# Two blocks of mixers and MLPs: the second layers' modulation vectors from VectorE, GpSimd and ScalarE instead of TensorE

## The chip, the cores and the metric

The kernel runs on one core of a Trainium2 chip. The metric is the time of one execution on the device in microseconds (us). Engines are named as in the profile: PE is TensorE, with PEld for its weight loads; DVE is VectorE, ACT ScalarE, POOL GpSimd; SP is the engine whose queue issues nearly all DMA loads.

## The reference, cut to what matters

There are two blocks of two layers each, on 256 tokens and 256 context tokens of width 1024. Every layer has a mixer and a squared-ReLU MLP (1024 to 4096 to 1024), each behind an RMS norm whose result is scaled and shifted by a modulation vector; another part of that vector scales what is added to the residual. Each layer has its own modulation matrix of 1024 x 6144, applied to two vectors: c for the tokens and c_ctx for the context.

```python
def modulation(cvec, w_mod, b_mod):
    m = (jax.nn.silu(cvec) @ w_mod + b_mod).reshape(-1, 1, N_MOD * D_MODEL)
    return jnp.split(m, N_MOD, axis=-1)

sh1, sc1, g1, sh2, sc2, g2 = modulation(c, w_mod[l], b_mod[l])
csh1, csc1, cg1, csh2, csc2, cg2 = modulation(c_ctx, w_mod[l], b_mod[l])
...
x = x + g1 * heads_out(att_x, px, hy, w_out[l])
x = x + g2 * sq_relu_mlp(modulate(rms_norm(x, norm2_g[l]), sh2, sc2), w_mlp1[l], w_mlp2[l])
```

The second block does the same with `ada_w`, `ada_b` and c_2, c_ctx_2; its first mixer is a gated DeltaNet, its second gated linear attention (GLA). In the last layer of each block only the tokens go through the MLP, so there are two MLPs with both streams (512 columns) and two with one (256 columns).

## The kernel before

The residual `xs` stays in SBUF, feature by feature, 8 tiles of 128 x 512 (tokens, then context). All large products are made in three passes of rounded fp32: a weight tile `wr` of 128x1024 comes by DMA, ACT rounds it to `wh` (line 296), DVE or POOL subtracts to get the rest `wl` (line 297), and PE multiplies wh by both parts of the input and wl by the first (lines 305 to 307). A weight has three buffers `wr`.

An MLP has four slabs. A slab takes eight weights up (each gives 128 hidden rows `h`: a relu on ACT from PSUM, a multiply on DVE for the square, then `pair` splits it into two rounded tiles `r` by an ACT cast and a DVE subtraction) and eight weights down, whose products are added to `xs` times the modulation (line 619). So an MLP has 64 weights. The weights' subtractions are on DVE, but for the first four, which are on POOL. The first products of an MLP with two streams begin while the norm of the second stream is still being made.

A modulation matrix is worked off in 48 steps (six groups of 1024 columns, eight slices of 128 rows each). A step loads 128x1024 values (`wm`, 512 KB) and has PE multiply them with silu(c) and silu(c_ctx) into PSUM `pmd`, four matmuls side by side in the array (line 365). After eight steps ACT copies the sums (`ev`), two more matmuls turn them feature-major and DVE adds the bias into `mod` (`moda` for the first block, `modb` for the second). The steps stand in a list; `pools` gives each stage a quota of them, and `background(n)` in the stages' code takes n of them. With four matrices there are 192 steps: 48 in layer 0's mixer, 24 in its MLP (10 ahead of the first products), 48 in layer 1's mixer (some run while its MLP begins), none in that MLP itself, 40 in DeltaNet (as 80 half steps: ten around the first heads and 70 in and behind the last head), 16 in the MLP behind DeltaNet and 16 in GLA.

A scheduler puts the instructions of each engine in an order at build time; at run time each engine works off its own list in order, and waits for what an instruction needs.

## Time and profile before

| what | value |
|---|---|
| three runs | 2713.63, 2722.64, 2725.65 us; median 2722.64 |
| profiled execution, first to last instruction (its span) | 2721.8 us |
| PE, DVE, ACT, POOL busy | 95%, 60%, 42%, 14% of the span |
| mean granted TensorE clock | 0.982 of full speed |
| DMA | 334 MB, mean 123 GB/s |
| first MLP with two streams | about 317 to 715 us |
| DeltaNet | about 1115 to 1935 us |
| second MLP with two streams | about 1935 to 2300 us |

The profile gives the execution's span; its time as a run isn't listed apart. The span lies 0.8 us below the median of the runs. Busy shares are means over stages of different kinds.

### The profile page before, as it was taken

The numbers are of one execution on the slowest core, as the hardware profiler recorded it, in microseconds if no ns is written. First come the engines' busy times: TensorE is split into PE (matmuls) and PEld (weight loads), VectorE is DVE, ScalarE is ACT, GpSimd is POOL, SyncE is SP. The second block draws the span as 40 slices with busy tenths as digits, with TensorE's granted clock in tenths as the row PEclk, the third lists the DMA queues.
The fourth block names the chain that finished last, engine by engine and source line by source line (L and its number), as shares of the span: only waits on it lengthen the run. The fifth ranks groups of instructions, "written<-read, shape, count | busy, mean of one in ns | idle before, by whom it ended". The sixth has DMA issues, their size and how long they took to land.

```text
span 2721.8 us, 41263 instructions
## 1 busy us (share of the span) xinstructions
PE 2583.2 (95%) x15900; PEld 2131.4 (78%) x15900; DVE 1629.2 (60%) x3455; ACT 1138.5 (42%) x2165; POOL 367.6 (14%) x270
## 2 busy tenths in 40 slices
PE   7999999999999999889999999999999999899999
PEld 5866777888866899867777787766778888687999
DVE  5554543344653678778776776775534445767675
ACT  3344332223443445545444444433422333563453
POOL 0000200000100101233232333322000002410100
PEclk9999999999999999999999999999999999999999
DMA  7234453223455656231112112236542222233554
GB/s 275 95 113 151 157 176 100 94 94 100 149 180 169 233 182 198 87 103 48 38 58 63 50 39 61 70 113 200 179 132 93 98 96 88 93 125 101 174 183 155
DMA packets 155205, 334.16 MB, mean 123 GB/s; under 512 B 60110, under 2 KB 71488, under 8 KB 155008
## 3 DMA queue, kind: packets, MB, share of 16 engines
q1 hardware_dynamic: 154752, 331.46, 37.3%
q8 instruction: 125, 2.05, 0.3%
q14 instruction: 72, 0.59, 0.1%
q0 software_dynamic: 256, 0.07, 0.0%
HBM read 327.79 MB, written 3.67 MB: 122 GB/s over the span
## 4 chain that ended last, share of the span: by engine, by line
PE 78%; DVE 13%; ACT 3%; DMA 3%; issue 2%; POOL 1%; SPq 0%; DVEq 0%; ACTq 0%
PE pmm L305 18%; PE pmm L306 18%; PE pmm L307 18%; PE pmd L365 3%; PE pt L986 1%; PE ps L958 1%; DVE lf L1211 1%; PE pv L994 1%; DMA wm<-amod 1%; PE pa L1280 1%; PE pa L1323 1%; PE pmm L324 1%; DVE Mt L1191 1%; PE pa L1275 1%; PE pa L1269 1%
## 5 line engine op out<-in xcount | busy, mean ns | idle before, releaser
L296 ACT CAST wh<-wr 128x1024 fp32r<-128x1024 f32 (+1 forms) x421 | 426.3, 1016 | 740.8 <-PE pmm L306 530.9
L305 PE MATMUL pmm<-h,wh 128*128 128x512 f32 (+2 forms) x1800 | 630.7, 351 | 18.2 <-DVE kq L1123 8.2
L307 PE MATMUL pmm<-h,wl 128*128 128x512 f32 (+2 forms) x1800 | 626.8, 348 | 14.3 <-DVE wl L297 9.4
L306 PE MATMUL pmm<-h,wh 128*128 128x512 f32 (+2 forms) x1800 | 627.2, 349 | 0.0
L297 DVE TENSOR_TENSOR wl<-wr,wh 128x1024 fp32r<-128x1024 f32 (+1 forms) x333 | 394.3, 1186 | 304.2 <-ACT wh L296 295.9
L305 PE MATMUL pmm<-r,wh 128*128 128x256 f32 (+1 forms) x1312 | 446.0, 341 | 11.6 <-DVE xs L619 10.1
L307 PE MATMUL pmm<-r,wl 128*128 128x256 f32 (+1 forms) x1312 | 444.1, 339 | 5.3 <-DVE wl L297 5.2
L306 PE MATMUL pmm<-r,wh 128*128 128x256 f32 (+1 forms) x1312 | 441.6, 337 | 0.4 <-DVE r L284 0.4
L297 POOL TENSOR_TENSOR wl<-wr,wh 128x1024 fp32r<-128x1024 f32 x88 | 214.2, 2437 | 1574.5 <-ACT wh L296 1169.5
L305 PEld LDWEIGHTS pmm<-h,wh 128*128 128x128 f32 x1800 | 343.6, 191 | 72.8 <-issue 11.3
L307 PEld LDWEIGHTS pmm<-h,wl 128*128 128x128 f32 x1800 | 345.0, 192 | 63.6 <-DVE wl L297 11.5
L306 PEld LDWEIGHTS pmm<-h,wh 128*128 128x128 f32 x1800 | 344.4, 191 | 46.0 <-issue 4.4
L305 PEld LDWEIGHTS pmm<-r,wh 128*128 128x128 f32 x1312 | 247.6, 189 | 53.8 <-issue 25.5
L307 PEld LDWEIGHTS pmm<-r,wl 128*128 128x128 f32 x1312 | 247.9, 189 | 30.7 <-DVE wl L297 6.1
L306 PEld LDWEIGHTS pmm<-r,wh 128*128 128x128 f32 x1312 | 248.2, 189 | 23.3 <-issue 1.6
L619 DVE SCALAR_TENSOR_TENSOR xs<-pmm,modb,xs 128x256 f32<-128x256 f32 x232 | 107.3, 478 | 127.2 <-PE pmm L307 126.9
L365 PE MATMUL pmd<-wm,cvs 128*32 128x256 f32 x1408 | 124.4, 394 | 10.3 <-DMA wm<-amod 7.0
L619 DVE SCALAR_TENSOR_TENSOR xs<-pmm,moda,xs 128x256 f32<-128x256 f32 x120 | 54.5, 479 | 130.1 <-PE pmm L307 130.0
L283 ACT CAST r<-h 128x256 fp32r<-128x256 f32 (+1 forms) x128 | 65.6, 514 | 135.8 <-DVE h L572 75.6
L284 DVE TENSOR_TENSOR r<-h,r 128x256 fp32r<-128x256 f32 (+1 forms) x128 | 72.7, 569 | 42.5 <-ACT r L283 39.8
L365 PEld LDWEIGHTS pmd<-wm,cvs 128*32 128x32 f32 x1408 | 36.4, 109 | 62.1 <-issue 25.6
L323 PE MATMUL pmm<-h,wh 128*128 128x256 f32 x224 | 63.7, 296 | 5.5 <-ACT h L480 3.8
(483 smaller groups left out, 3837.8 us busy)
## 6 DMA issues: line engine op xcount, KB each, us to landing
wr<-w SPq DMA_DIRECT2D x128, 512.0 KB
wr<-f SPq DMA_DIRECT2D x128, 512.0 KB
wm<-wmod SPq DMA_DIRECT2D x96, 512.0 KB
wm<-amod SPq DMA_DIRECT2D x56, 512.0 KB
wr<-dwin SPq DMA_DIRECT2D x49, 512.0 KB
...
```

The lines of the kernel that those rows point to most:

```text
L283: self.nc.scalar.copy(hi, src)
L284: self.nc.vector.tensor_tensor(lo, src, hi.bitcast(F32), ALU.subtract)
L296: self.nc.scalar.copy(hi, raw)
L297: (self.nc.gpsimd if pool or self.pool_lo else self.nc.vector).tensor_tensor(lo, raw, hi.bitcast(F32), ALU.subtract)
L305: mm(ps, wh[:, k, :], rh[:, n0:n1], start=k == 0, stop=False)
L306: mm(ps, wh[:, k, :], rl[:, n0:n1], start=False, stop=False)
L307: mm(ps, wl[:, k, :], rh[:, n0:n1], start=False, stop=k == last)
L323: mm(ps[:, c0:c1], wh[:, k, :], rh[:, c0:c1], start=k == 0, stop=False)
L324: mm(ps[:, c0:c1], wh[:, k, :], rl[:, c0:c1], start=False, stop=False)
L365: self.last = nc.tensor.matmul(ps[32 * c : 32 * c + 32, :256], cs[:, k, :], raw[:, 256 * j : 256 * j + 256], start=k == 0, stop=k == 7, ti ...
L619: self.nc.vector.scalar_tensor_tensor(x, ps, mod[:, 8 * gch + m, v : v + 1], x, ALU.mult, ALU.add)
L958: mm(ps[:, nk * i : nk * i + nk], q[:, C(b)], kp[hh % 2][:, k0:], start=True, stop=True)
```

## The change

The modulation matrices of the two second layers (`wmod_1` and `amod_1`) are laid out transposed on the host: 48 tiles of 128 output features by 1024 inputs. c and c_ctx are laid out repeated over the 128 partitions (`cb`, 2 x 1024 columns, put through Silu once on ACT). For each of the 48 tiles POOL multiplies it by silu(c_ctx) into a product `pr`, which ACT sums along its columns; DVE multiplies it by silu(c) and sums in one instruction (`jk` is its discarded product). Every eighth tile DVE adds the bias. This goes on during the two MLPs with two streams: `vec()` takes one tile after each hidden row block and after each of the first three slabs' down products. 96 steps on PE remain for the first layers' matrices: 48 in layer 0's mixer, 10 in its MLP ahead of the first products, 38 in layer 1's mixer; DeltaNet, the second MLP and GLA have none.

```diff
+def _rows(w):
+    return _c(w.T.reshape(48, P, 1024))
...
+    def modulation_v(self, wname, bname, cname, tag):
+        nc = self.nc
+        mod = self.cp.tile([P, 48, 2], F32, name="mod" + tag, tag="mod" + tag)
+
+        def steps():
+            cb = self.t("cb", 2048)
+            nc.sync.dma_start(cb, self.a[cname])
+            nc.scalar.activation(cb, cb, AF.Silu)
+            raws = []
+
+            def load(j):
+                raw = self.gp.tile([P, 1024], F32, tag="wm", bufs=self.nwm, name="wm")
+                nc.sync.dma_start(raw, self.a[wname][j])
+                raws.append(raw)
+
+            def total(j, prod):
+                nc.scalar.activation(prod, prod, AF.Copy, accum_out=mod[:, j, 1:2])
+                if j % 8 == 7:
+                    m = mod[:, j - 7 : j + 1, :]
+                    nc.vector.tensor_tensor(m, m, self.small(bname)[:, j - 7 : j + 1].unsqueeze(2).to_broadcast([P, 8, 2]), ALU.add)
+
+            late = None
+            for j in range(self.nwm):
+                load(j)
+            for j in range(48):
+                yield
+                raw = raws.pop(0)
+                prod = self.t("pr", 1024)
+                nc.gpsimd.tensor_tensor(prod, raw, cb[:, 1024:], ALU.mult)
+                jk = self.t("jk", 1024)
+                nc.vector.scalar_tensor_tensor(jk, raw, 1.0, cb[:, :1024], ALU.mult, ALU.mult, accum_out=mod[:, j, 0:1])
+                if j + self.nwm < 48:
+                    load(j + self.nwm)
+                if late:
+                    total(*late)
+                late = (j, prod)
+            yield
+            total(*late)
+
+        return mod, steps
...
+    def vec(self, n=1):
+        for _ in range(n):
+            if self.vs and next(self.vs, 0) == 0:
+                self.vs = None
...
+            if vs:
+                sb.update(cb=(1, 2048), jk=(1, 1024), pr=(2, 1024))
...
             ws = [self.weight(self.a[w1][m], pool=True) for m in range(4)]
             self.background(head)
+            self.vs = vs() if vs else None
...
                     hid.append(self.pair(t, n))
                     self.background(1)
+                    self.vec()
...
             if not S:
                 self.background(1)
+                self.vec()
...
-                            mods2.extend(self.modulation(f"amod_{j}", f"abmod_{j}", "cv2", f"b{j}") for j in range(2))
-                            self.bg = self.bg + mods[1][1] + mods2[0][1] + mods2[1][1]
+                            mods2.append(self.modulation("amod_0", "abmod_0", "cv2", "b0"))
+                            mods2.append(self.modulation_v("amod_1", "abmod_1", "cvr2", "b1"))
+                            self.bg = self.bg + mods2[0][1]
...
-                        self.quota = 48
+                        self.quota = 38
...
-                    self.ffn(xs, "g2_0", "w1_0", "w2_0", mods[0][0], "2_0", both, ys, None, 24, 10, S, None, before, lambda sv: f["then"](sv))
+                    self.ffn(xs, "g2_0", "w1_0", "w2_0", mods[0][0], "2_0", both, ys, None, 10, 10, S, None, before, lambda sv: f["then"](sv),
+                             mods[1][1])
...
-            self.quota = 40
...
-        self.ffn(xs, "fg_0", "f1_0", "f2_0", mods2[0][0], "4", both, None, h, 16, 0, S, None, before, lambda sv: f["then"](sv))
+        self.ffn(xs, "fg_0", "f1_0", "f2_0", mods2[0][0], "4", both, None, h, 0, 0, S, None, before, lambda sv: f["then"](sv),
+                 mods2[1][1])
...
-            self.pools(st, sb, dict(gt=2, ad=2, po=1, md=1, mm=2), 4, "gt", 16, nwm=2)
+            self.pools(st, sb, dict(gt=2, ad=2, po=1, md=1, mm=2), 4, "gt", nwm=2)
```

The rows that follow are lists of instructions as built; the line numbers are each kernel's own. DVE at the start of the first MLP with two streams, before the change, from the norm's last tiles on:

```order
L477 SCALAR_TENSOR_TENSOR h<-n,moda_116,h 128x256 x2
L297 TENSOR_TENSOR wl<-wr,wh 128x1024
L572 TENSOR_TENSOR h<-h,pmm 128x512 x3
L284 TENSOR_TENSOR r<-h,r 128x512
L297 TENSOR_TENSOR wl<-wr,wh 128x1024
L284 TENSOR_TENSOR r<-h,r 128x512
L572 TENSOR_TENSOR h<-h,pmm 128x512
L284 TENSOR_TENSOR r<-h,r 128x512
L297 TENSOR_TENSOR wl<-wr,wh 128x1024
L284 TENSOR_TENSOR r<-h,r 128x512
```

DVE at the same place in the changed kernel, from the norm's last tile on (`jk` is the new multiply-and-sum, `moda_117` the second layer's vector):

```order
L537 SCALAR_TENSOR_TENSOR h<-n,moda_116,h 128x256
L425 SCALAR_TENSOR_TENSOR jk,moda_117<-wm,cb 128x1024 x8
L414 TENSOR_TENSOR moda_117<-moda_117,bmod_163 128x16
L425 SCALAR_TENSOR_TENSOR jk,moda_117<-wm,cb 128x1024 x2
L637 TENSOR_TENSOR h<-h,pmm 128x512 x3
L308 TENSOR_TENSOR wl<-wr,wh 128x1024
L295 TENSOR_TENSOR r<-h,r 128x512
L308 TENSOR_TENSOR wl<-wr,wh 128x1024
L295 TENSOR_TENSOR r<-h,r 128x512
L637 TENSOR_TENSOR h<-h,pmm 128x512
L295 TENSOR_TENSOR r<-h,r 128x512
L308 TENSOR_TENSOR wl<-wr,wh 128x1024
```

Eleven `jk` (the first one stands just ahead of these rows) now stand between the norm and the first hidden row's multiply. Behind that, up to the last of the 48, 37 `jk` stand among 19 `wl`; in the second MLP it is 4 ahead, and 44 among 22 `wl`.

POOL from the first MLP's first weights to its last slab, before the change:

```order
L297 ISA
L297 TENSOR_TENSOR wl<-wr,wh 128x1024 x4
L481 TENSOR_TENSOR h<-n,h 128x256 x8
L297 TENSOR_TENSOR wl<-wr,wh 128x1024 x2
L481 TENSOR_TENSOR h<-n,h 128x256 x8
```

and in the changed kernel (`pr` is the product with silu(c_ctx)):

```order
L308 TENSOR_TENSOR wl<-wr,wh 128x1024 x4
L541 TENSOR_TENSOR h<-n,h 128x256 x7
L423 TENSOR_TENSOR pr<-wm,cb 128x1024
L541 TENSOR_TENSOR h<-n,h 128x256
L423 TENSOR_TENSOR pr<-wm,cb 128x1024 x47
L308 TENSOR_TENSOR wl<-wr,wh 128x1024 x2
```

POOL's 48 multiplies begin behind its seventh tile of the norm and stand next to each other.

PE in the merge of DeltaNet's last head (`pa` are the merge's products, `pmd` the modulation's), before the change:

```order
L1275 MATMUL pa<-Y,FT 128x128 x4
L1280 MATMUL pa<-FT,Y 128x128 x4
L1269 MATMUL pa<-TT,Mt 128x128 x4
L365 MATMUL pmd<-wm,cvs 32x256 x5
L1275 MATMUL pa<-Y,FT 128x128 x4
L1280 MATMUL pa<-FT,Y 128x128 x4
L1269 MATMUL pa<-TT,Mt 128x128 x4
L365 MATMUL pmd<-wm,cvs 32x256 x7
L1275 MATMUL pa<-Y,FT 128x128 x4
```

and in the changed kernel:

```order
L1342 MATMUL pa<-Y,FT 128x128 x4
L1347 MATMUL pa<-FT,Y 128x128 x4
L1336 MATMUL pa<-TT,Mt 128x128 x4
L1342 MATMUL pa<-Y,FT 128x128 x4
L1347 MATMUL pa<-FT,Y 128x128 x4
L1336 MATMUL pa<-TT,Mt 128x128 x4
L1342 MATMUL pa<-Y,FT 128x128 x4
L1347 MATMUL pa<-FT,Y 128x128 x4
```

The products of the merge keep their order, and the modulation's matmuls between them are gone.

## Rows read from the trace of the kernel before

**Rows 1.** The page: busy time of each engine in us, share, instructions.
```profile
PE 2583.2 (95%) x15900; PEld 2131.4 (78%) x15900; DVE 1629.2 (60%) x3455; ACT 1138.5 (42%) x2165; POOL 367.6 (14%) x270
```

**Rows 2.** Busy us (instructions) by stretch, all engines; then PE's modulation matmuls alone.
```profile
430.00:720.00 290.00, 288.25 (x1373) 240.18 (x1371) 129.08 (x210) 92.98 (x137) 11.15 (x10) 1.00 0.29 95
2010.00:2300.00 290.00, 287.08 (x1347) 236.71 (x1343) 128.49 (x202) 89.74 (x127) 10.70 (x15) 0.99 0.28 93
...
895.00:1112.00 217.00, 5.10 (x64) 1.67 (x64) 0.99 0.59 195
```

**Rows 3.** ACT's timeline, the relus of both MLPs: start us, length, instruction, count.
```profile
360.33 1.56 ACT L571 ACTIVATE h<-pmm 128x512 f32<-128x512 f32 x3
...
444.54 0.59 ACT L571 ACTIVATE h<-pmm 128x512 f32<-128x512 f32 x1
...
483.60 0.59 ACT L571 ACTIVATE h<-pmm 128x512 f32<-128x512 f32 x1
...
2069.16 0.59 ACT L571 ACTIVATE h<-pmm 128x512 f32<-128x512 f32 x1
```

**Rows 4.** Line 297 (ns min/median/max), then POOL's and DVE's timelines at 911.
```profile
L297 DVE TENSOR_TENSOR wl<-wr,wh x333: 408/1225/3356, 45.0 to 2710.7; 128x1024 fp32r<-128x1024 f32 x155, 128x384 fp32r<-128x384 f32 x8, 128x256 fp32r<-128x256 f32 x4
L297 POOL TENSOR_TENSOR wl<-wr,wh x88: 2337/2402/2813, 308.1 to 2536.3; 128x1024 fp32r<-128x1024 f32 x88
...
911.34 2.36 POOL L297 TENSOR_TENSOR wl<-wr,wh 128x1024 fp32r<-128x1024 f32 x1 [0.52 <-ACT wh L296]
...
911.42 3.36 DVE L297 TENSOR_TENSOR wl<-wr,wh 128x1024 fp32r<-128x1024 f32 x1
```

**Rows 5.** DVE: xs updates (min/median/max), then groups by shape (busy us, mean ns | idle).
```profile
L619 DVE SCALAR_TENSOR_TENSOR xs<-pmm,modb,xs x232: 467/477/497, 1298.9 to 2718.3; 128x256 f32<-128x256 f32 x116
...
L284 DVE TENSOR_TENSOR r<-h,r 128x512 fp32r<-128x512 f32 x64 | 44.2, 690 | 37.0 <-ACT r L283 37.0
L572 DVE TENSOR_TENSOR h<-h,pmm 128x512 f32<-128x512 f32 x64 | 43.2, 680 | 1.0 <-ACT h L571 1.0
...
L1123 DVE SCALAR_TENSOR_TENSOR vf<-pmm,dcw,vf 128x508 f32<-128x508 f32 x32 | 23.8, 743 | 20.1 <-ACT vf L1118 19.8
```

**Rows 6.** POOL's and DVE's timelines at 2395; POOL's multiplies and subtractions of 256 columns.
```profile
2395.83 2.12 POOL L1525 TENSOR_TENSOR kE<-kE,k 128x256 f32<-128x256 f32 x1 [2.15 <-ACT kE L1522]
...
2395.06 2.29 DVE L1563 TENSOR_TENSOR LV<-LV,q 128x2048 f32<-128x2048 f32 x1 [0.77 <-ACT LV L1562]
...
L1525 POOL TENSOR_TENSOR kE<-kE,k x8: 724/1060/2121, 2350.0 to 2441.8; 128x256 f32<-128x256 f32 x8
...
L481 POOL TENSOR_TENSOR h<-n,h x28: 725/740/1480, 332.1 to 2306.7; 128x256 fp32r<-128x256 f32 x28
```

**Rows 7.** Chain that ended last, by line: 1780 to 1945, 2305 to 2505, 715 to 915.
```profile
by line: PE pmd L365 13.1%; PE pmm L305 6.7%; PE pa L1323 5.1%; PE pmm L306 5.0%; PE pmm L307 5.0%; DMA wm<-amod 4.9%; PE pa L1305 4.1%; PE pmm L324 4.0%; PE pmm L325 3.7%; SPq L1227 3.6%; PE pa L1312 3.6%; PE pmm L323 3.5%; PE pa L1280 3.0
...
by line: PE pmm L1499 6.6%; DVE cum L1455 6.6%; PE pmm L1498 6.5%; PE pmm L1497 6.5%; PE pmm L307 6.5%; PE pmm L306 5.8%; PE pmm L305 5.8%; DMA wm<-amod 5.1%; PE pad L1583 4.7%; PE pmd L365 4.0%; DVE LV L1559 3.2%; DVE LV L1558 3.1%; PE pgt
...
by line: PE pmd L365 11.6%; PE pmm L305 11.2%; PE pmm L306 10.7%; PE pmm L307 10.6%; PE ps L958 7.5%; PE pt L986 7.3%; PE pv L994 6.0%; DMA wm<-amod 3.7%; DMA cv<-cv 2.8%; PE pmm L928 2.7%; issue 2.3%; DMA wr<-w 2.1%; DVE wl L297 2.0%; PE p
```

**Rows 8.** ACT's groups by shape: accumulator reads, a pass of 2048 columns, table loads.
```profile
L963 ACT ACTIVATION_READ_ACCUMULATOR E<-ps,smx,rq 128x1 f32 x48 | 9.4, 195 | 0.0
...
L1562 ACT ACTIVATE LV<-LV 128x2048 f32<-128x2048 f32 x8 | 15.2, 1913 | 5.4 <-DVE rst L401 3.2 <-DVE LV L1558 2.2
...
L1124 ACT ACT_TABLE_LOAD x10 | 12.8, 1283 | 0.2
```

**Rows 9.** Timelines: POOL's seventh norm tile (first MLP), ACT's last cast (second).
```profile
342.26 0.73 POOL L481 TENSOR_TENSOR h<-n,h 128x256 fp32r<-128x256 f32 x1 [0.46 <-ACT h L480]
...
1933.14 0.39 ACT L480 CAST h<-e 128x256 fp32r<-128x256 f32 x1
```

**Rows 10.** Busy time by stretch, all engines, then PE's granted clock, DMA share, GB/s.
```profile
330.00:333.00 3.00, 2.97 (x18) 1.86 (x17) 2.44 (x9) 1.98 (x5) 0.73 (x1) 0.50 0.61 224
```

**Rows 11.** The chain in order of time, a wait for a load.
```profile
323.45 4.77 DMA wm<-wmod
```

More of the change, by code (lines that the diff above doesn't have):

```diff
@@ L136, in host_arrays @@
     a["cv2"] = _c(np.stack([i["c_2"][0], i["c_ctx_2"]], 0).reshape(2, 8, P).transpose(2, 1, 0))
+    for n, c, cc in (("cvr", "c", "c_ctx"), ("cvr2", "c_2", "c_ctx_2")):
+        a[n] = _c(np.broadcast_to(np.concatenate([i[c][0], i[cc]])[None], (P, 2048)))
     for l in range(2):
@@ L139, in host_arrays @@
         a[f"g2_{l}"] = _fm(i["norm2_g"][l])
-        a[f"wmod_{l}"] = _moving(i["w_mod"][l])
+        if l == 0:
+            a["wmod_0"] = _moving(i["w_mod"][0])
+            a["amod_0"] = _moving(i["ada_w_2"][0])
+        else:
+            a["wmod_1"] = _rows(i["w_mod"][1])
+            a["amod_1"] = _rows(i["ada_w_2"][1])
         a[f"bmod_{l}"] = _fm(i["b_mod"][l])
@@ L166, in host_arrays @@
         a[f"w2_{l}"] = _slabs(i["w_mlp2"][l])
-        a[f"amod_{l}"] = _moving(i["ada_w_2"][l])
         a[f"abmod_{l}"] = _fm(i["ada_b_2"][l])
@@ L380, in modulation @@
         return mod, [s for cc in range(6) for s in steps(cc)]
+    def modulation_v(self, wname, bname, cname, tag):
[36 more added lines that the diff above has]
+            if self.vs and next(self.vs, 0) == 0:
+                self.vs = None
     def gscale(self, mod, ch, gname, tag):
@@ L514, in residual, with ffn @@
                                                 xs[:, m, c0:c1], ALU.mult, ALU.add)
-    def ffn(self, xs, g, w1, w2, mod, tag, streams, ys=None, h=None, quota=0, head=0, S=None, scales=None, before=None, then=None):
+    def ffn(self, xs, g, w1, w2, mod, tag, streams, ys=None, h=None, quota=0, head=0, S=None, scales=None, before=None, then=None, vs=None):
         one = len(streams) == 1
         with ExitStack() as st:
-            self.pools(st, dict(n=(8, 256), h=3, acc=(4, 256), sq=(4, 256), rs=(1, 258)), dict(a=2, md=1, mm=5), 12 if one else 18, "a", quota)
+            sb = dict(n=(8, 256), h=3, acc=(4, 256), sq=(4, 256), rs=(1, 258))
+            if vs:
+                sb.update(cb=(1, 2048), jk=(1, 1024), pr=(2, 1024))
+            self.pools(st, sb, dict(a=2, md=1, mm=5), 12 if one else 18, "a", quota)
             self.wp2 = self.lo
@@ L533, in ffn @@
             self.background(999)
+            self.vec(999)
             self.wp2 = None
@@ L1663, in run @@
                         next(filt)
-                        mods = [self.modulation(f"wmod_{j}", f"bmod_{j}", "cv", f"a{j}") for j in range(2)]
+                        mods = [self.modulation("wmod_0", "bmod_0", "cv", "a0"), self.modulation_v("wmod_1", "bmod_1", "cvr", "a1")]
                         self.bg = mods[0][1]
@@ L1765, in run @@
             self.sel = self.const("k_sel")
-            mods2 = [self.modulation(f"amod_{l}", f"abmod_{l}", "cv2", f"b{l}") for l in range(2)]
+            mods2 = [self.modulation("amod_0", "abmod_0", "cv2", "b0"), self.modulation_v("amod_1", "abmod_1", "cvr2", "b1")]
             with ExitStack() as st:
-                self.bg = mods2[0][1] + mods2[1][1]
+                self.bg = mods2[0][1]
                 self.pools(st, dict(acc=1, sq=3), dict(a=2, md=1), 2, "a", 64)
```

## The prediction

> **What bounds the kernel now.** I began with the page. TensorE (PE) is busy 95% of the span, VectorE (DVE) 60%, ScalarE (ACT) 42% and GpSimd (POOL) 14% [rows 1]. So it looks as if any matmul that leaves PE were won and the other engines had room. An average over stages doesn't settle that, so I read the table by stage next. In the two-stream MLPs PE is busy 288 of 290 us (430 to 720) and 287 of 290 (2010 to 2300), while DVE is busy 129 and 128 there and POOL 11 [rows 2]. A weight of 128x1024 costs PE 5.58 us: the relus of weights 16 to 23 (counted from 0) of the first MLP start from 444.54 to 483.60, seven steps of 5.58 [rows 3]. For each such weight ACT rounds it (wh) and DVE subtracts (wl, 1.22 us, [rows 4]). As long as DVE delivers a wl each 5.58 us, PE is the bound; 1.22 plus 0.69 and 0.68 for r and h [rows 5] is far from that.
>
> Then I looked for what happens when POOL and DVE work together, since the change sets them side by side. At 911.34 a POOL subtraction starts (2.36 us, to 913.70). The DVE subtraction wl that starts at 911.42 lasts 3.36 instead of 1.22 and ends 1.08 after POOL's [rows 4]. It goes the other way too: POOL's multiply of 128x256 at 2395.83, alone 0.72, lasts 2.12, to 0.60 after the DVE instruction with two SBUF operands that had begun at 2395.06 [rows 6]. The xs update, whose one operand lies in PSUM, lasts 0.467 to 0.497 wherever it runs [rows 5]. So of a POOL instruction that reads SBUF and a DVE instruction with two SBUF operands one waits for the whole of the other, but for some 0.12 to 0.15 us of its own start: 1.22 - 1.08 = 0.14 for DVE, 0.72 - 0.60 = 0.12 for POOL.
>
> The Trainium skill, page "SBUF — State Buffer", section "Who interferes with whom", calls this an exclusive lock on a port pair that the two engines share, held for a whole instruction, and counts DVE instructions with two SBUF inputs among those that take it. By that rule, with full durations and no overlap of the starts, the two stages below would last some 13 us longer each, which gives 2836 us; the rows show the 0.12 to 0.15 and decide.
>
> **The change part by part.**
>
> *What comes off PE.* 96 of 192 modulation steps. The eight that run behind 895 cost PE 5.1 us, 0.64 each [rows 2]. The first MLP loses 14, the second 16, 19 us, both contained in the stage sums below. Elsewhere I take the chain of work that ended last [rows 7]:
> - DeltaNet's last head (1780 to 1945): pmd matmuls 13.1% of 165 us = 21.6, waits for the wm loads 4.9% = 8.1. The merge between those matmuls alternates between two halves, so much of what they cover is covered by the other half; but DVE's latency comes up in part. 24, bounds 15 and 29.7. The ten half steps near 1200 are five whole ones, 3.2 us, in a stage where DVE is busy as well: 2, bounds 0 and 3.2.
> - GLA (2305 to 2505): 4.0% of 200 = 8.0, loads 5.1% = 10.2. 12, bounds 6 and 18.2.
> - Layer 1's mixer and the start of its MLP lose ten steps, 6.4 us; on the chain of 715 to 915 there are also waits for loads (3.7% of 200) and for reloading c where the two blocks' steps alternate (2.8%), 13 us. 11, bounds 6.4 and 19.
> Sum: 49 us saved, bounds 27 and 71.
>
> *What comes on.* In each two-stream MLP 48 steps: a POOL multiply of 128x1024 with both operands in SBUF, a DVE multiply-and-add (jk) with both operands in SBUF, an ACT sum. POOL: 2.40 us, the median of its subtractions of this shape [rows 4]; multiply and subtract of 256 have the same lowest time, 0.72 and 0.73 [rows 6]. DVE: no row has this shape; 256 columns take 0.477 and 508 take 0.743 [rows 5], 1.055 ns a column, so 1024 take 1.29 (estimate). Its accumulator: on ACT reading one out costs 0.195 [rows 8], on DVE no row shows it; bounds 0 and 0.195, I take 0.1. ACT: less than the 1.91 of its row of 2048 columns, and 0.19 [rows 8], so under 101 us in all; ACT is busy 93 of 290 us there [rows 2], so that is hidden.
>
> Both multiplies need the operand that excludes the other. A step therefore costs (2.40 - 0.12) + (1.29 - 0.14) = 3.43 us that nothing with two SBUF operands can share, wl and r included. And the order puts the steps ahead of the weights' subtractions: in the first MLP DVE has 11 jk ahead of the first relu's multiply, then 37 more among 19 wl; in the second 4, then 44 among 22. DVE works in order, so a wl waits for every jk ahead of it and each jk for a POOL multiply.
>
> First MLP, from the first multiply to the last jk: 48 x 3.43 = 164.6; 19 wl x 1.08 = 20.5; 11 r x 0.55 = 6.1; sum 191. DVE's work without a second SBUF operand (11 h x 0.68 + 16 xs x 0.48 = 15.2) hides beneath POOL's multiplies or not: half, 7.6. Accumulators 4.8. Together 203.6, bounds 191 and 216. POOL's multiplies start behind its seventh norm tile, at 343.0 [rows 9]. So the next weight's wl (the 24th weight) is there at 343.0 + 203.6 + 1.2 = 547.8. Before, PE began that weight at 478.0 (its relu's start less 5.58, [rows 3]). From then on nothing of the new work is left, so the stage ends 70 us later, bounds 57 and 82; the removed steps are in that, since 478.0 holds them.
>
> Second MLP: 164.6 + 22 x 1.08 + 14 x 0.55 = 196; half of 14 x 0.68 + 16 x 0.48 = 17.2 is 8.6; accumulators 4.8; 209.4, bounds 196 and 223. The start: the norm's last ACT cast ends at 1933.5 [rows 9], then the copy of c through Silu, 2048 columns: 1.91 by ACT's row of that width, 1.28 for a table [rows 8], 1936.7. The 27th weight's wl comes at 1936.7 + 209.4 + 1.2 = 2147.3. Before, PE began it two weights after the 24th's end: 2069.16 + 2 x 5.58 = 2080.3 [rows 3]. So 67 us later, bounds 54 and 80.
>
> The sum: +70 + 67 - 49 = +88 us on the profiled execution's span of 2721.8, which lies 0.8 below the median of the runs: **2810 us**. With all bounds together: +40 to +135.
>
> PE's clock: it ran at 0.50 of full speed between 330 and 333, behind a wait for a load [rows 10], and PE will wait between weights here. At half speed a weight would take 11.2 us, the stretch gives 203.6/19 = 10.7 for each. So the lower level costs some 10 us a stage at most.
>
> **The rivals.**
> *The steps hide (faster).* POOL needs 48 x 2.40 = 115 us and DVE 48 x 1.29 = 62, and each alone fits into an MLP's 64 x 5.58 = 357 us. For it speaks the average load. If POOL's multiply and DVE's work ran side by side, the ten products ahead of the first relu would cost 343.0 + 24 + 1.2 - 360.3 = 8 us [rows 3, 9], and the rest be saved: 2722 - 19 - 49 + 8 = 2662. Against it stand the rows at 911 and 2395. The point that decides is the cost of a step: the stages lose as much as is saved elsewhere if they lose 25 us each, 45 less than above, which is 0.94 a step. Up to 2.6 us a step the change is no loss. The Trainium skill, page "Perfetto Trace Analysis", section "Optimizing Scalar/DVE Operations", warns that moving work between VectorE and GpSimd might not help because of the shared port; by that it comes out on the other side of 2.6.
> *The loads become the bound (slower still).* Three wm buffers serve POOL and DVE; one returns after both have read it, then a load of 512 KB took 4.77 us from its issue [rows 11]. (2.4 + 1.3 + 4.8)/3 = 2.8 us a step, below 3.5; but SP's queue is in order, wm and weight loads alternate in it, and each waits for its buffer. At 4.2 us a step: 48 x 0.7 x 2 = 67 more, 2877.
>
> **How the numbers follow.** Lock at its measured price, 2810: 0.70. Steps hidden, 2662: 0.14. Break-even around 2.6 us a step, near 2722: 0.05. Loads or queue order on top, above 2860: 0.11. By 0.5% (13.6 us), about what a measurement of this kernel tells from no change: faster 0.16, same 0.04, slower 0.80. The range from 2735 to 2880 leaves out the hidden case and half of break-even; the forecast's own bounds are 2762 to 2857.
>
> **What would show it.** In the two MLPs: wl and jk on DVE at 2 to 4 us instead of 1.2, PE waiting for wl in most weights of the first slabs, the stages some 70 us longer, PE's share there far below 99%. jk at 1.3 us beside running multiplies, or POOL's multiplies spread thinly, would refute it. In DeltaNet's last head and in GLA no pmd, and these stages some 24 and 12 us shorter. The number is wrong if DVE and POOL don't exclude each other in this form, or if the 48 steps take clearly less or more than 200 us.

## The result, and the profile after

The changed kernel takes **2839.07 us** (median; 2833.91 to 2841.56) against 2723.02 before: a ratio of 1.0426, 95% interval 1.0399 to 1.0453. The forecast was 2810, slower, in a range from 2735 to 2880. The profiled execution spans 2838.2 us, 116.4 more than before.

The page's busy times come first, then the stretches of [rows 2] and the stretch in which the first MLP's 48 steps lie (columns as in [rows 2]: length, busy us and instructions of PE, PEld, DVE, ACT, POOL, then granted clock, DMA share, GB/s).

```profile
PE 2560.8 (90%) x15084; PEld 2138.1 (75%) x15084; DVE 1917.0 (68%) x3647; ACT 1240.7 (44%) x2341; POOL 648.7 (23%) x362
```

```profile
430.00:720.00 290.00, 259.87 (x1069) 208.34 (x1070) 189.87 (x198) 99.70 (x141) 76.42 (x27) 0.94 0.41 127
2010.00:2300.00 290.00, 234.07 (x911) 182.45 (x911) 229.29 (x220) 113.26 (x171) 122.85 (x43) 0.89 0.48 148
...
343.00:575.00 232.00, 166.42 (x712) 132.83 (x712) 215.86 (x190) 99.12 (x158) 145.05 (x50) 0.84 0.54 165
```

Over the span VectorE still looks free at 68%. In the stretch of the steps TensorE works 166 of 232 us and VectorE 216. VectorE's timeline from 351 (accumulator reads left out) and GpSimd's beside it show with what:

```profile
351.49 3.29 DVE L425 SCALAR_TENSOR_TENSOR jk<-wm,cb 128x1024 f32<-128x1024 f32 x1
...
354.82 3.29 DVE L425 SCALAR_TENSOR_TENSOR jk<-wm,cb 128x1024 f32<-128x1024 f32 x1
...
358.15 3.29 DVE L425 SCALAR_TENSOR_TENSOR jk<-wm,cb 128x1024 f32<-128x1024 f32 x1
...
347.78 15.87 POOL L423 TENSOR_TENSOR pr<-wm,cb 128x1024 f32<-128x1024 f32 x5
```

Five multiplies run back to back on GpSimd for 15.87 us, and beside each a jk lasts 3.29 us. All jk of both MLPs, then the multiplies and the weights' subtractions of the first (ns min/median/max, first and last start):

```profile
L425 DVE SCALAR_TENSOR_TENSOR jk<-wm,cb x48: 1208/3235/3447, 343.8 to 539.4; 128x1024 f32<-128x1024 f32 x48
...
L425 DVE SCALAR_TENSOR_TENSOR jk<-wm,cb x48: 1209/1226/3487, 1991.1 to 2194.8; 128x1024 f32<-128x1024 f32 x48
...
L423 POOL TENSOR_TENSOR pr<-wm,cb x48: 2340/3223/3466, 343.6 to 538.9; 128x1024 f32<-128x1024 f32 x48
...
L308 DVE TENSOR_TENSOR wl<-wr,wh x24: 1208/1225/3399, 382.9 to 556.6; 128x1024 fp32r<-128x1024 f32 x24
```

A jk alone takes 1.21 us and a multiply alone 2.34 (the shortest of each); together the pair takes 3.3. A median says little here, since most instructions are either free or held until the other engine's is done: that of the second MLP's jk is 1.226, its longest 3.487. The chain of waits of 343 to 560 has a trap for the reader:

```profile
by line: issue 33.5%; DVE jk L425 29.6%; DVE wl L308 12.3%; DMA wm<-wmod 7.3%; DVE h L637 3.6%; DVE r L295 3.5%; ACT wh L307 1.9%; DVE xs L686 1.9%; DVE gs L446 1.4%; POOL pr L423 1.2%; DVE h L537 0.8%; PE pmm L317 0.7%; ACT r L294 0.6%; AC
...
351.52 3.19 issue
```

A third of it is "issue", where no releaser is shown. The piece at 351.52 is the jk of 351.49, which runs beside a multiply: the profile infers releasers from semaphores and names none for it. GpSimd's multiply stands there with 1.2%.

The relus that answer to [rows 3], the first ones, weights 16 and 23 of the first MLP, then the third slab's first of either MLP:

```profile
377.85 1.07 ACT L636 ACTIVATE h<-pmm 128x512 f32<-128x512 f32 x2
...
505.90 0.58 ACT L636 ACTIVATE h<-pmm 128x512 f32<-128x512 f32 x1
...
556.44 0.59 ACT L636 ACTIVATE h<-pmm 128x512 f32<-128x512 f32 x1
607.17 0.60 ACT L636 ACTIVATE h<-pmm 128x512 f32<-128x512 f32 x1
...
2249.55 0.59 ACT L636 ACTIVATE h<-pmm 128x512 f32<-128x512 f32 x1
```

Where the 116 us arose, by marks that both traces have:

| mark | before | after | later by | this part | forecast |
|---|---|---|---|---|---|
| first MLP, third slab's first relu | 532.73 | 607.17 | 74.4 | +74.4 | +70 |
| second MLP, its norm's last cast on ACT | 1933.14 | 1982.81 | 49.7 | -24.8 | -37 (11 + 2 + 24) |
| second MLP, third slab's first relu | 2118.30 | 2249.55 | 131.3 | +81.6 | +67 |
| end of the span | 2721.8 | 2838.2 | 116.4 | -14.9 | -12 |

### The profile page after: what moved, and what is told of

Same layout as the page of the kernel before. It is cut to its first block, busy times and chain, and to the rows that moved or that the text cites. A ratio compares the mean times of both kernels' runs of the same rounds, so it can differ in the third digit from the quotient of the medians.

```text
span 2838.2 us, 40176 instructions
## 1 busy us (share of the span) xinstructions
PE 2560.8 (90%) x15084; PEld 2138.1 (75%) x15084; DVE 1917.0 (68%) x3647; ACT 1240.7 (44%) x2341; POOL 648.7 (23%) x362
## 4 chain that ended last, share of the span: by engine, by line
PE 63%; DVE 23%; issue 6%; ACT 4%; DMA 4%; POOL 1%; SPq 0%; DVEq 0%; ACTq 0%; POOLq 0%
PE pmm L316 15%; PE pmm L317 14%; PE pmm L318 14%; DVE jk L425 4%; DVE wl L308 3%; DVE xs L686 1%; PE pmd L376 1%; DMA wm<-wmod 1%; PE pv L1061 1%; PE ps L1025 1%; PE pt L1053 1%; DVE lf L1278 1%; PE pa L1347 1%; ACT wh L307 1%; DVE r L295 1%
## 5 line engine op out<-in xcount | busy, mean ns | idle before, releaser
L318 PE MATMUL pmm<-h,wl 128*128 128x512 f32 (+2 forms) x1800 | 641.0, 356 | 63.4 <-DVE wl L308 57.4
L316 PE MATMUL pmm<-h,wh 128*128 128x512 f32 (+2 forms) x1800 | 639.7, 355 | 42.9 <-ACT wh L307 21.0
L317 PE MATMUL pmm<-h,wh 128*128 128x512 f32 (+2 forms) x1800 | 636.3, 354 | 0.0
L308 DVE TENSOR_TENSOR wl<-wr,wh 128x1024 fp32r<-128x1024 f32 (+1 forms) x333 | 428.8, 1289 | 217.0 <-ACT wh L307 205.1
L316 PE MATMUL pmm<-r,wh 128*128 128x256 f32 (+1 forms) x1312 | 452.0, 346 | 41.5 <-ACT r L294 33.9
L317 PE MATMUL pmm<-r,wh 128*128 128x256 f32 (+1 forms) x1312 | 450.1, 343 | 14.2 <-DVE r L295 14.2
L316 PEld LDWEIGHTS pmm<-h,wh 128*128 128x128 f32 x1800 | 352.4, 196 | 93.9 <-ACT wh L307 33.7
L317 PEld LDWEIGHTS pmm<-h,wh 128*128 128x128 f32 x1800 | 352.7, 196 | 45.2 <-issue 0.8
L316 PEld LDWEIGHTS pmm<-r,wh 128*128 128x128 f32 x1312 | 252.1, 193 | 80.1 <-ACT r L294 39.2
L423 POOL TENSOR_TENSOR pr<-wm,cb 128x1024 f32<-128x1024 f32 x96 | 284.1, 2978 | 120.4 <-DMA wm<-amod 54.4
L317 PEld LDWEIGHTS pmm<-r,wh 128*128 128x128 f32 x1312 | 252.8, 193 | 44.5 <-DVE r L295 20.0
L425 DVE SCALAR_TENSOR_TENSOR jk<-wm,cb 128x1024 f32<-128x1024 f32 x96 | 220.8, 2301 | 10.2 <-ACT cb L402 7.6
L411 ACT ACTIVATE pr<-pr 128x1024 f32<-128x1024 f32 x96 | 101.7, 1059 | 167.1 <-POOL pr L423 166.9
L295 DVE TENSOR_TENSOR r<-h,r 128x256 fp32r<-128x256 f32 (+1 forms) x128 | 96.1, 752 | 33.2 <-ACT r L294 30.6
```

Of the source, the lines that this page charges most:

```text
L295: self.nc.vector.tensor_tensor(lo, src, hi.bitcast(F32), ALU.subtract)
L308: (self.nc.gpsimd if pool or self.pool_lo else self.nc.vector).tensor_tensor(lo, raw, hi.bitcast(F32), ALU.subtract)
L316: mm(ps, wh[:, k, :], rh[:, n0:n1], start=k == 0, stop=False)
L317: mm(ps, wh[:, k, :], rl[:, n0:n1], start=False, stop=False)
L318: mm(ps, wl[:, k, :], rh[:, n0:n1], start=False, stop=k == last)
L411: nc.scalar.activation(prod, prod, AF.Copy, accum_out=mod[:, j, 1:2])
```

## The experiments

The theory to be tested, **lock**: GpSimd's multiply and a VectorE instruction with two SBUF operands exclude each other, and that sets the time. The rivals: **queue** (jk is slow by itself and stands ahead of the weights in VectorE's order; GpSimd has no part), and **loads** (three wm buffers and SP's order set the pace). A third, **sums**, came out of the first four runs: ScalarE's sums wait for GpSimd's products, and the roundings wh behind them come late. All are edits of the changed kernel. The kernel before took 2717 to 2720 us beside them. The numbers of instructions are for each of the two MLPs. Differences of 6 to 9 us are at the limit of what these runs tell apart: the intervals of such a pair overlap or touch, though no run of the one lies within the range of the other.

| kernel | GpSimd multiply | jk on VectorE | ACT sums | us | ratio to before (95%) | above "no steps" |
|---|---|---|---|---|---|---|
| no steps | no | no | no | 2662.0 | 0.978 (0.977 to 0.980) | 0 |
| both products on VectorE | no | 96 | no | 2668.0 | 0.981 (0.979 to 0.983) | 6 |
| no GpSimd multiply | no | 48 | yes | 2675.8 | 0.983 (0.981 to 0.985) | 14 |
| GpSimd multiply alone | 48 | no | no | 2726.1 | 1.002 (1.001 to 1.003) | 64 |
| no jk | 48 | no | yes | 2741.1 | 1.008 (1.006 to 1.010) | 79 |
| paced, no sums | 48 | 48, one a weight | no | 2698.7 | 0.992 (0.989 to 0.995) | 37 |
| paced | 48 | 48, one a weight | yes | 2742.6 | 1.009 (1.007 to 1.012) | 81 |
| no sums | 48 | 48 | no | 2830.0 | 1.040 (1.038 to 1.041) | 168 |
| the change | 48 | 48 | yes | 2839.1 | 1.043 (1.040 to 1.045) | 177 |

**Both products on VectorE.**

```diff
-                nc.scalar.activation(prod, prod, AF.Copy, accum_out=mod[:, j, 1:2])
...
-                prod = self.t("pr", 1024)
-                nc.gpsimd.tensor_tensor(prod, raw, cb[:, 1024:], ALU.mult)
+                prod = None
...
+                jk = self.t("jk", 1024)
+                nc.vector.scalar_tensor_tensor(jk, raw, 1.0, cb[:, 1024:], ALU.mult, ALU.mult, accum_out=mod[:, j, 1:2])
```

> Both products of a step on VectorE (96 jk in each two-stream MLP instead of 48), none on GpSimd; the ScalarE sum goes too. Theory lock (GpSimd's multiply and a VectorE instruction with two SBUF operands exclude each other): a step costs VectorE 2 x 1.22 plus two accumulators, about 2.6 us, instead of the 3.3 us from jk to jk in the changed kernel, and wl and r are back at 1.22 and 0.69. VectorE's order now has 96 jk among some 34 weights in the first MLP: 123 + 34 x 1.22 + 18 x 1.37 + 32 x 0.48 = 205 us of VectorE for 190 us of TensorE, some 15 to 30 us lost in each MLP instead of 74 and 82, so about 2740 us (2700 to 2790), faster than the changed kernel although VectorE does twice the products. Theory queue (jk is slow by itself, about 2.3 us, and VectorE's order makes the weights wait; GpSimd has no part in it): 48 more jk of 2.3 us in each MLP, 2839 + 2 x 110 = about 3060 us; at 1.22 us each still above 2900. Theory loads (the three wm buffers and SP's order set the pace): unchanged, 2820 to 2850.

Measured 2667.96 us: faster than the changed kernel by 171 and than the kernel before by 52, with twice the jk. Queue and loads fall. The direction is the lock's, but its number, 2740, was too high by 72, and the measured time lies below its range (2700 to 2790). It counted 15 to 30 us lost in each MLP, because VectorE has 205 us of work for TensorE's 190; what is lost is 6 us in both together, against the kernel without steps. That explains up to 54 of the 72; where the rest went wrong isn't on record. The stretch of the steps and one line of jk:

```profile
343.00:575.00 232.00, 230.38 (x1071) 190.85 (x1070) 208.90 (x329) 70.35 (x90) 1.30 (x1) 1.00 0.65 199
...
L423 DVE SCALAR_TENSOR_TENSOR jk<-wm,cb x48: 1214/1224/1227, 342.5 to 536.5; 128x1024 f32<-128x1024 f32 x48
```

VectorE is as busy as in the changed kernel (209 and 216 us), TensorE works 230 of 232 us. Busy VectorE isn't the harm; held VectorE is.

**One multiply left out.** In the first kernel the sum reads the weight itself (`activation(prod, raw, ...)`). In the second jk is gone, and the bias line takes the context's sums for both vectors:

```diff
-                nc.gpsimd.tensor_tensor(prod, raw, cb[:, 1024:], ALU.mult)
```

```diff
-                nc.vector.scalar_tensor_tensor(jk, raw, 1.0, cb[:, :1024], ALU.mult, ALU.mult, accum_out=mod[:, j, 0:1])
```

> GpSimd's multiply is left out: ScalarE sums the weight itself, so the modulation of the context stream in both second layers is not the reference's. VectorE's jk, the loads, the buffers and ScalarE's sums stay. Theory lock: jk at 1.22 us wherever it runs; VectorE has 48 x 1.28 + 19 x 1.22 + 11 x 1.37 + 16 x 0.48 = 107 us for the 19 weights that cost TensorE 106 us, so each MLP loses at most the 10 or 12 jk ahead of the first relu (10 us): 2670 to 2700 us. Theory queue: VectorE's work and order are nearly unchanged, so is the time, 2810 to 2850. Theory loads: a step still needs its load of 4.8 us through three buffers, at least (1.3 + 4.8 + 1.1)/3 = 2.4 us a step, and some 20 us lost in each MLP: 2710 to 2740.

> VectorE's multiply-and-add (jk) is left out: the modulation of the main stream in both second layers takes the context's value. GpSimd's multiplies, the loads and ScalarE's sums stay. Theory lock: GpSimd's 48 multiplies take 115 to 130 us in each MLP and hold up each wl and r behind at most one of them: in the first half of a slab 3.4 + 2.9 + 0.68 = 7.0 us a weight instead of 5.58, in the second half 3.4 + 1.0, hidden; some 10 to 20 us lost in each MLP: 2680 to 2720. So neither multiply alone costs much, only the two together do. Theory queue: without jk nothing is ahead of the weights: 2660 to 2680, and wl stays at 1.22 us. Theory loads: 2710 to 2740.

Without GpSimd's multiply 2675.78, as the lock says (2670 to 2700); jk are at 1.21 to 1.23 us. Without jk 2741.11, outside what I had expected (2680 to 2720): with no jk beside them GpSimd's multiplies, their loads and the sums cost 79 us, 65 more than jk with loads and sums do. "Neither alone costs much" fell.

**Paced.** VectorE's order in the change has 48 jk among the first 19 or 22 weights. Here each jk stands behind the last VectorE instruction of the weight after which it is written (r or the xs update), so that there is one for a weight:

```diff
-        self.nc.vector.tensor_tensor(lo, src, hi.bitcast(F32), ALU.subtract)
+        self.lastd = self.nc.vector.tensor_tensor(lo, src, hi.bitcast(F32), ALU.subtract)
...
-                nc.vector.scalar_tensor_tensor(jk, raw, 1.0, cb[:, :1024], ALU.mult, ALU.mult, accum_out=mod[:, j, 0:1])
+                with self.tc.issue_after(self.lastd.ins):
+                    nc.vector.scalar_tensor_tensor(jk, raw, 1.0, cb[:, :1024], ALU.mult, ALU.mult, accum_out=mod[:, j, 0:1])
...
-        self.nc.vector.scalar_tensor_tensor(x, ps, mod[:, 8 * gch + m, v : v + 1], x, ALU.mult, ALU.add)
+        self.lastd = self.nc.vector.scalar_tensor_tensor(x, ps, mod[:, 8 * gch + m, v : v + 1], x, ALU.mult, ALU.add)
```

> The changed kernel with one edit: each jk is put behind the last VectorE instruction of the weight after which it is written (r, or the xs update), so that VectorE has one jk for each of 48 weights instead of 48 among 19 or 22. Theory lock: per weight of the first half of a slab 2.35 + 1.22 + 1.22 + 0.69 less some 0.27 of overlaps = 5.2 us of the shared operand path, below TensorE's 5.58; in the second half 4.5. So the steps fit, but r of a slab's last weight can wait for one multiply at each change of half (some 2.5 us, three times in each MLP), 2670 to 2715 us, faster than both kernels. Theory queue: about 2668, with wl and r at 1.22 and 0.69. Theory loads: the loads have 5.58 us each as well; 2668 to 2700. If the lock costs more than its instructions last (GpSimd starved, a wait chain through wm and pr), 2750 or more.

2742.62: 96 us better than the change, but above the ranges of all three theories (the highest ends at 2715) and nearest to the expectation's last case, a chain through wm and pr (2750 or more). The chain of waits at 563 shows that one, and in it a link that I hadn't counted:

```profile
562.91 1.22 DVE jk L426 x2
...
564.18 3.33 DMA wm<-wmod
...
567.65 3.23 POOL pr L423
...
570.90 0.02 ACT pr L411
570.93 0.94 issue
...
572.06 0.95 ACT wh L307
...
573.03 2.95 DVE wl L308
```

A jk frees a buffer, the load follows, then the multiply, then ScalarE's sum (ACT pr and the "issue" behind it), and behind the sum in ScalarE's order the next weight's rounding wh, without which neither wl nor the matmuls can begin. So the theory of the sums was formed. It was tested by leaving them out of three kernels, the change, the one without jk and the paced one; a fourth has no steps at all, nor their loads. The line that goes:

```diff
-                nc.scalar.activation(prod, prod, AF.Copy, accum_out=mod[:, j, 1:2])
```

> The changed kernel without ScalarE's sums of GpSimd's products (the context stream's modulation takes the main stream's value). GpSimd's multiplies, jk and the loads stay. Theory lock: VectorE was busy 99% of the stretch and sets its length, so little changes: 2790 to 2840. Theory sums (ScalarE works in order, its sums wait for GpSimd's products, and the weights' roundings wh behind them reach VectorE and TensorE late; that, not the lock, is the loss): about 2690, as without GpSimd's multiply.

> The kernel without jk, now without ScalarE's sums as well: only GpSimd's 96 multiplies and the loads are left of the steps (both streams' modulation comes from single products, not from sums). With jk alone out the kernel took 2741. Theory lock: wl and r still wait behind GpSimd's multiplies, in the first half of a slab 7.0 us a weight: 2710 to 2745. Theory sums: the 65 us above the kernel without GpSimd's multiply (2676) came from ScalarE's sums waiting for products and loads; without them 2660 to 2690.

> The paced kernel (one jk for each of 48 weights) without ScalarE's sums (the context stream's modulation takes the main stream's value). With the sums it took 2743. Theory sums: each sum stands in ScalarE's order ahead of a weight's rounding and waits for a product that waits for a load issued a weight earlier; without the sums the paced steps fit, 2670 to 2690. Theory lock: the multiply and what it excludes on VectorE take 5.2 us of each 5.58, and any lateness stays: 2715 to 2745.

> The changed kernel without any of the 96 steps (both second layers' modulation is the bias alone): what the removal from TensorE is worth by itself. The prediction's terms: 49 saved outside the two MLPs and 19 in them, 2722 - 68 = 2654. By the trace of the changed kernel 25 and 15 were saved outside the MLPs, and 19 in them if nothing replaced them: 2722 - 59 = 2663. If the missing matmuls let the clock of TensorE fall and give their time back, 2690 or more.

The change without sums: 2829.98, so they are worth 9 us of its 177, and the lock's expectation holds. Without jk: 2726.11, the sums 15 of 79, again in the lock's range. Paced: 2698.69, the sums 44 of 81, between the two ranges. GpSimd waits for its loads as long in the paced kernel without sums as with them (152 and 156 us between 343 and 700), so what was won there isn't that wait. Both causes are real: the lock wherever GpSimd's multiply runs, the sums on top where VectorE is no longer the slowest. Removal alone: 2662.03, where the trace had said 2663 and the prediction's terms 2654. How GpSimd's multiply alone costs time, 64 us in all, is seen on VectorE in the kernel that has nothing else of the steps but their loads and the bias (VectorE's timeline, then GpSimd's):

```profile
369.33 3.40 DVE L308 TENSOR_TENSOR wl<-wr,wh 128x1024 fp32r<-128x1024 f32 x1
372.65 2.87 DVE L295 TENSOR_TENSOR r<-h,r 128x512 fp32r<-128x512 f32 x1
375.45 0.67 DVE L634 TENSOR_TENSOR h<-h,pmm 128x512 f32<-128x512 f32 x1
376.05 2.30 DVE L295 TENSOR_TENSOR r<-h,r 128x512 fp32r<-128x512 f32 x1
378.27 3.42 DVE L308 TENSOR_TENSOR wl<-wr,wh 128x1024 fp32r<-128x1024 f32 x1
...
368.82 21.26 POOL L422 TENSOR_TENSOR pr<-wm,cb 128x1024 f32<-128x1024 f32 x7
```

wl lasts 3.4 instead of 1.22, r 2.3 to 2.9 instead of 0.69, and h, whose second operand lies in PSUM, its 0.67. A weight in the first half of a slab needs one of each: 7 us, as long as the multiplies run back to back, where TensorE needs 5.58.

**The operands.** First jk's factor is put into PSUM, in two banks that the norm's and the products' tiles give up; then, in another kernel, GpSimd's multiply gets one operand instead of two.

```diff
+            cp = self.cps.tile([P, 1024], F32, tag="cp", name="cp")
+            nc.scalar.copy(cp[:, :512], cb[:, :512])
+            nc.scalar.copy(cp[:, 512:], cb[:, 512:1024])
...
-                nc.vector.scalar_tensor_tensor(jk, raw, 1.0, cb[:, :1024], ALU.mult, ALU.mult, accum_out=mod[:, j, 0:1])
+                nc.vector.scalar_tensor_tensor(jk, raw, 1.0, cp, ALU.mult, ALU.mult, accum_out=mod[:, j, 0:1])
...
-            self.pools(st, sb, dict(a=2, md=1, mm=5), 12 if one else 18, "a", quota)
+            self.pools(st, sb, dict(a=1 if vs else 2, md=1, mm=4 if vs else 5), 12 if one else 18, "a", quota)
...
```

```diff
-                nc.gpsimd.tensor_tensor(prod, raw, cb[:, 1024:], ALU.mult)
+                nc.gpsimd.tensor_scalar(prod, raw, 1.0, None, ALU.mult)
```

> The changed kernel with one operand of jk moved: the 1024 values of silu(c) that jk multiplies by lie in PSUM (two banks, one taken from the norm's and one from the products' tiles), so that jk has one SBUF operand, as the xs update has. GpSimd's multiplies and ScalarE's sums stay. Theory lock by two SBUF operands: jk 1.2 to 1.35 us wherever it runs; left are the waits of wl and r behind the multiplies and the sums, as in the kernel without jk (2741), and jk's own 60 us of VectorE in each MLP: 2745 to 2785. Theory lock by any VectorE work beside GpSimd's multiply: jk stays at 2.3 us and the time at 2820 to 2850.

> The changed kernel with GpSimd's multiply of two SBUF operands replaced by a multiply of one SBUF operand by the constant 1 (the context stream's modulation is then the plain sum of the weights); the order on VectorE is the same, instruction for instruction. If what excludes VectorE is GpSimd's second operand: jk and wl fall to 1.22 us beside it, 2700 to 2750, the rest being the sums. If any GpSimd instruction that reads SBUF excludes it for as long as it lasts: what decides is how long the form with one operand lasts; at the same 2.35 us the time stays at 2820 to 2850.

The first took 2752.30 us, the second 2738.32 (1.012 and 1.007 of before). The groups of the first MLP, jk and multiply of the PSUM kernel:

```profile
L428 DVE SCALAR_TENSOR_TENSOR jk<-wm,cp x48: 1203/1208/1223, 347.2 to 500.9; 128x1024 f32<-128x1024 f32 x48
...
L426 POOL TENSOR_TENSOR pr<-wm,cb x48: 2340/2409/3398, 347.0 to 497.1; 128x1024 f32<-128x1024 f32 x48
```

and of the kernel with one operand on GpSimd, with a stretch of the two timelines:

```profile
L425 DVE SCALAR_TENSOR_TENSOR jk<-wm,cb x48: 1211/1226/2060, 341.8 to 494.1; 128x1024 f32<-128x1024 f32 x48
...
L423 POOL TENSOR_SCALAR pr<-wm x48: 2763/2878/3832, 341.6 to 494.1; 128x1024 f32<-128x1024 f32 x48
...
442.28 1.23 DVE L308 TENSOR_TENSOR wl<-wr,wh 128x1024 fp32r<-128x1024 f32 x1 [0.74 <-ACT wh L307]
443.42 2.06 DVE L425 SCALAR_TENSOR_TENSOR jk<-wm,cb 128x1024 f32<-128x1024 f32 x1
...
436.81 33.36 POOL L423 TENSOR_SCALAR pr<-wm 128x1024 f32<-128x1024 f32 x11
```

With one operand in PSUM no jk of either MLP lasts over 1.223 us, whatever GpSimd does: for jk the exclusion belongs to the second SBUF operand, as the forecast read it from the xs update. It isn't so for all of VectorE's instructions. In the changed kernel a `tensor_scalar` with one SBUF operand of 128x16, 0.17 us alone, is held behind a multiply too (VectorE's timeline, then GpSimd's):

```profile
419.06 2.31 DVE L446 TENSOR_SCALAR gs<-moda 128x16 f32<-128x16 f32 x1
...
415.69 15.58 POOL L423 TENSOR_TENSOR pr<-wm,cb 128x1024 f32<-128x1024 f32 x5 [5.92 <-DMA wm<-wmod]
```

On GpSimd's side the multiply by a constant, which has one SBUF operand, doesn't hold VectorE for its length: beside eleven of them, back to back for 33.36 us, VectorE's instructions of 1024 columns with two SBUF operands last from 1.22 to 2.06 us.

The times of both kernels stay near that of the kernel without jk, which has the same sums and loads. In the one with one operand on GpSimd 101 of the 177 us come back, though VectorE's order, the sums and the loads are those of the change. What holds the other 76 was not taken apart. The trace has GpSimd at work there almost without a pause (48 instructions, 147.2 us, with 7.7 us between them in the first MLP), so that its own pace, through the wm buffers and the sums, is the nearest candidate.

The Trainium skill, page "SBUF — State Buffer", section "Who interferes with whom", says that a VectorE instruction with two SBUF inputs contends with a GpSimd instruction that reads SBUF. For GpSimd's form with two operands the traces agree (3.4 us for wl); for that with one operand they show 0.88 us of delay at most for a jk (2.09 - 1.21), not a wait for its 2.9.

**What the last DeltaNet head lost with its steps.** Its pmd were forecast to be worth 24 us; the head became some 5 shorter. TensorE's granted clock fell at the start of its merge: 0.50 from 1880 to 1885 in the changed kernel, the lower level (1.2 GHz), behind 5 us in which TensorE was busy for 1.65 and waited for the block inverses' load. To see whether the clock ate the gain, matmuls that nobody reads were put behind each group of the merge, on top of the kernel with both products on VectorE:

```diff
+            def fill(mmi):
+                if hd == 7:
+                    with self.tc.issue_after(mmi.ins):
+                        ps, cs = self.p("md"), self.silu_c("cv2")
+                        for i in range(2):
+                            mm(ps[:32, :256], cs[:, 0, :], Mt[:, 0].rearrange("p v i -> p (v i)"), start=True, stop=True)
...
+                    fill(z)
...
```

> The kernel with both products on VectorE (2668), and 32 matmuls of 32x256 that nobody reads put into the last DeltaNet head's merge on TensorE, two behind each group of the merge's own, where 24 half steps of the modulation used to run. Theory clock (without those steps TensorE idles between the merge's groups, its granted clock falls to half there and the groups take 2.1 instead of 1.1 us): the clock stays at 1.00 in the merge and the head ends up to 5 us earlier than without them: 2660 to 2668. Theory latency (the merge is held by VectorE's subtractions and copies between the groups, and by the loads and the state steps behind it; the clock is a by-product): unchanged or up to 8 us later, 2665 to 2677.

2689.91 us, 22 more than without and outside both ranges (2660 to 2668, 2665 to 2677). Two stretches of the merge with the filler (busy of the engines, then the clock):

```profile
1802.00:1812.00 10.00, 10.00 (x59) 6.28 (x58) 3.45 (x5) 1.14 (x2) 0.00 (x0) 1.00 0.00 0
1812.00:1822.00 10.00, 10.00 (x59) 6.28 (x58) 3.45 (x5) 0.27 (x1) 0.00 (x0) 1.00 0.01 2
```

From 1802 on the clock is at 1.00 (0.83 from 1792 to 1802, where the merge begins). But TensorE is busy all of the time there, since the filler is dearer than the steps were (four of its matmul records in 1.05 us at 1806.35, ten of the old ones in 1.05 at 1839.22 in the trace before): from the first to the last of its subtractions on VectorE the merge takes 29.7 us, where it takes 20.4 in the kernel without filler. So the run doesn't tell what the clock is worth. And of the 24 us by which the spans differ only 10 had arisen by the second MLP's norm; the rest arose in that MLP, where VectorE's order came out differently (14 jk ahead of the first relu's multiply instead of 5).

The traces set a bound. The merge's first multiplies on VectorE, in the kernel before and in the changed one:

```profile
1824.71 0.69 DVE L1271 TENSOR_TENSOR Y<-pa,lm 128x512 f32<-128x512 f32 x1 [4.12 <-PE pa L1269]
...
1829.40 0.69 DVE L1271 TENSOR_TENSOR Y<-pa,lm 128x512 f32<-128x512 f32 x1
...
1880.12 0.69 DVE L1338 TENSOR_TENSOR Y<-pa,lm 128x512 f32<-128x512 f32 x1 [6.96 <-PE pa L1336]
...
1888.31 0.69 DVE L1338 TENSOR_TENSOR Y<-pa,lm 128x512 f32<-128x512 f32 x1 [0.96 <-PE pa L1336]
...
1892.26 0.69 DVE L1338 TENSOR_TENSOR Y<-pa,lm 128x512 f32<-128x512 f32 x1 [0.29 <-PE pa L1336]
```

From the first to the second it is 4.69 us before, at a clock of 1.00, and 8.19 in the changed kernel, at 0.50 and then 0.61; the next step takes 3.95 there, with the clock back at 1.00 from 1890 on. So in the merge the lower level goes with 3.5 us at most, of the 18.6 that the head fell short.

**Both products on VectorE, paced.** The two edits together.

> The kernel with both products on VectorE (2668), each pair of jk put behind the last VectorE instruction of the weight after which it is written, as in the paced kernel. The kernel without any steps took 2662, which is the floor. Per weight VectorE has 2 x 1.3 + 1.22 + 0.69 + 0.68 = 5.2 us in the first half of a slab and 4.8 in the second, below TensorE's 5.58, so both orders fit and what can be won is the 6 us of jk ahead of the first relus: 2660 to 2670. If r of a slab's last weight is held up by a pair of jk at each change of half (2.6 us, twelve times in both MLPs, as far as it isn't covered), 2670 to 2690.

2674.52 us (0.985 of before, 0.983 to 0.987): no gain over 2667.96, in the second of the expected ranges, but not for its reason. In the first MLP TensorE lost 6.4 us at the start, in one wait for a wl that stood behind eight jk (length, PE's busy us and matmuls, granted clock, DMA share, GB/s):

```profile
370.00:380.00 10.00, 5.84 (x26) 0.90 0.48 138
380.00:390.00 10.00, 7.79 (x22) 0.59 0.78 249
```

From 390 to 700 it was busy throughout, the slabs' changes of half included, and in the second MLP it lost 6.4 us between 1920 and 1940 and nothing from there to 2240. As scheduled, the two starts cost 1.6 and 6.0 us. So the best version found is both products on VectorE as scheduled, 52 us below the kernel before and 6 above the kernel without steps.

## Why the prediction was right, point by point

- **The lock and its price.** Right, and the step on which all rested; in all it came to +116.4 us instead of +88. A pair takes 3.3 us (forecast 3.43; jk alone 1.21 where 1.29 was estimated, the multiply 2.34 where 2.40 was taken). From the first jk to the end of the last are 343.8 to 542.7, 199 us (forecast 203.6), and 1991.1 to 2195.9, 205 us (209.4). With the measured lengths the forecast's sum gives 196 and 202 (estimate). Moving one product off GpSimd (the sums go with it) or one of jk's operands into PSUM (wl and r stay held) gives 171 and 87 us back. In two points the rule was worded otherwise than the runs show, though neither enters the sum: it took any GpSimd instruction that reads SBUF, and the multiply by a constant delays a jk by 0.88 us at most; and it took VectorE instructions with two SBUF operands, and a `tensor_scalar` with one is held as well.
- **The two MLPs: +74 and +82 instead of +70 and +67.** Two sizes. The second MLP's steps began late: silu(c)'s row is loaded on SP when the phase begins, and ScalarE waits 5.92 us for it, which the forecast had not counted:

```profile
1982.81 0.39 ACT L540 CAST h<-e 128x256 fp32r<-128x256 f32 x1
1989.12 1.92 ACT L402 ACTIVATE cb<-cb 128x2048 f32<-128x2048 f32 x1 [5.92 <-DMA cb<-cvr]
```

 And "from then on nothing of the new work is left" was too kind: behind the last jk the third slab's first relu came 64 us later in the first MLP and 54 in the second, where the forecast had 56 (532.73 - 478.0 + 1.2) and 39 (2118.30 - 2080.3 + 1.2). More than one weight was left over: the h of the rows before had waited behind the jk as well. In the first MLP h, wh and wl then followed one behind the other at 3.46 us a weight (wl at 542.74, 546.19, 549.65, 553.11 and 556.56), before the down products began at 559.1. TensorE stood idle for 4.2 us between 550 and 560 and for 7.9 between 2190 and 2210, and behind that its clock was granted in part at the lower level: from 560 to 570 it was busy throughout and did 35 matmuls where it does 46 at the upper one, 2.4 us (length, PE's busy us and matmuls, granted clock, DMA share, GB/s):

```profile
550.00:560.00 10.00, 5.77 (x21) 0.89 0.47 150
560.00:570.00 10.00, 10.00 (x35) 0.77 0.23 75
570.00:580.00 10.00, 10.00 (x46) 1.00 0.35 105
```

 Ahead of the last jk the clock (0.83 from 343.8 to 542.8) didn't set the length: VectorE was busy for 197.1 of these 199.0 us.

- **ScalarE's sums were costed at nothing**, since ScalarE had time. By average load it has (99 of 232 us), but it works in order, and its sums wait for products. In the change this is worth 9 us; once VectorE is freer, 15 to 44. That this error did no more harm to the forecast is luck: the lock hid it.
- **Savings elsewhere: 40 instead of 49.** GLA gave 14.9 (forecast 12). From the first MLP's third slab to the second MLP's norm 24.8 (37). The share of the last head was the term that failed: forecast 24 (bounds 15 and 29.7), measured 5.4 (VectorE's last lf starts 55.0 later than before, ScalarE's last cast 49.7). The pmd in the merge, 58 matmul records between the groups, had been hidden: from the first to the last of its subtractions 21.2 us before and 20.6 after. Those beside the state steps gave some 9 us, up to the first xs update behind them; 4 went again ahead of the merge and on the way to the norm. Reading a line's share of the chain as its worth was wrong where the chain only passes from one half of the merge to the other through it.
- **The rivals.** "The steps hide" fell in the change, and its rule is right in the kernel on VectorE alone: 2668 where the rival had 2662. "Loads": refuted as a bound of their own by both products on VectorE, with the same loads at 2668; as a link in a chain they count, as the paced kernel shows.
